# Dense experts: the products with the value rows' low halves move to the end of each output

## The chip, the cores and the metric

The kernel runs on one core of one Trainium2 chip. The metric is the device time of one execution in microseconds (us). The core has a matrix engine (TensorE, in the profile PE, with its weight loads as PEld), a vector engine (VectorE, DVE), an activation engine (ScalarE, ACT), a general engine (GpSimd, POOL) and an engine that issues transfers (SyncE, SP). Each works through its own queue in order, and semaphores tie the queues together.

## The reference

One inference step of a one-layer decoder: a prompt of 1024 tokens and 32 sample tokens go through attention, an RWKV mixer and a layer of 16384 single-neuron experts. The change concerns the experts (PEER), of which each token picks 16 for each of 8 heads:

```python
gate = jax.nn.softmax(top_s, axis=-1)
act = jax.nn.gelu(jnp.einsum('nd,nhkd->nhk', hb, expert_u[eid]).astype(jnp.float32), approximate=False)
return jnp.einsum('nhk,nhkd->nd', gate * act, expert_v[eid].astype(jnp.float32))
```

`eid` holds the 128 picked experts of each token. All data is float32.

## The kernel before

The layer's first half (projections, attention, RWKV) fills the first 1700 us or so and is not touched. For the experts the nine tiles of tokens (128 rows each, the last with the 32 sample tokens) are divided. Tiles 5, 6, 7 and the sample tile are *gathered*: for each picked expert GpSimd issues an indirect load of its rows (tile `row`), and VectorE multiplies and sums them. Tiles 0 to 4, 640 tokens, are *dense*: TensorE runs all 16384 experts over them, and a table of gates (`g`, zero where an expert is not picked) makes the result the same. Both streams run side by side, the gathered one with priority, the dense one as filling.

`dense` (line 1615) takes the experts in 128 blocks of 128, four blocks to a group (`NG`), so 32 groups. `hidden(b)` computes the hidden values of one block for all 640 tokens, 48 products with 320 columns, then gelu, gates, and a split into a high half `ch` and a low half `cl`. `values(grp, dh)` loads the value rows of the four blocks, for one half `dh` of the 1024 output columns: SP loads `v`, ACT casts it to the high half `vh`, and GpSimd (every eighth time VectorE) subtracts to get the low half `vl` (`split2`, line 1611). `v` has two buffers, `vh` and `vl` have five each. `output(grp, dh, tt)` adds the four blocks' products for one tile of tokens into one of four PSUM banks (`d`), and VectorE adds the bank to the accumulator `acc` (`dacc` in the profile). In a group come the hidden blocks, the values of the first half, five outputs, the values of the second half, and five more outputs. Float32 accuracy comes from three products per block, made by `mm3` (line 243): high by high, high by low, low by high:

```python
te.matmul(out, l[0], r[0], start=first, stop=False)   # ch by vh
te.matmul(out, l[0], r[1], start=False, stop=False)   # ch by vl
te.matmul(out, l[1], r[0], start=False, stop=last)    # cl by vh
```

The order of each engine's queue is not the order of the text: when the program is built, a planner with a table of expected durations puts at each step the most urgent instruction whose operands it expects to be ready into an engine's queue. Text order gives the urgency. The products of one output keep their order, since they add into the same bank. A buffer is handed on when the planner has seen its last reader, and the new writer waits for that reader on the chip. Almost every instruction of the kernel is recorded at line 196, a helper, so rows are told apart by their tiles.

Of the kernel before, what the change touches and what calls it, by code (L numbers as in the profile page):

```python
# [125 lines left out]
def _ap(t, offset, ap):  # L126
    return bass.AP(tensor=t.tensor, offset=t.offset + offset, ap=ap)
# [74 lines left out]
def tile_hybrid_step(ctx, tc, ins, outs):  # L202
# [3 lines left out]
    ve, sc, gp, te, sy = (_Metered(meter, n, e) for n, e in (("ve", nc.vector), ("sc", nc.scalar), ("gp", nc.gpsimd),  # L206
                                                               ("te", nc.tensor), ("sy", nc.sync)))
# [22 lines left out]
    def split(src, hi, lo, eng=None):  # L230

        sc.copy(hi, src)
        (eng or ve).tensor_tensor(lo, src, hi.bitcast(FT), op=OP.subtract)
# [9 lines left out]
    def mm3(out, l, r, first, last):  # L243

        if len(l) == 1:
            te.matmul(out, l[0], r[0], start=first, stop=last)
            return
        te.matmul(out, l[0], r[0], start=first, stop=False)
        te.matmul(out, l[0], r[1], start=False, stop=False)
        te.matmul(out, l[1], r[0], start=False, stop=last)  # L250
# [1360 lines left out]
    def split2(src, hi, lo, j):  # L1611
        sc.copy(hi, src)
        (gp if j in POOL_LO else ve).tensor_tensor(lo, src, hi.bitcast(FT), op=OP.subtract)

    def dense(pa, pp, acc, h2T, tiles):

        nt = len(tiles)
        n = 128 * nt
        NG = 4
        C_, V_, G_ = {}, {}, {}  # L1620
        gate2 = {}

        def hidden(b):
            uh = pa.tile([128, KD, 128], FR, tag="uh", name="uh", bufs=2)
            ul = pa.tile([128, KD, 128], FR, tag="ul", name="ul", bufs=2)
            for x in range(2):
                ks = slice(4 * x, 4 * x + 4)
                u = pa.tile([128, 4, 128], FT, tag="u", name="u", bufs=3)
                sy.dma_start(u, A["uT"][b, :, ks])
                split2(u, uh[:, ks], ul[:, ks], 8 + b % 2)  # L1630
            ch = pa.tile([128, n], FR, tag="ch", name="ch", bufs=NG + EARLY)
            cl = pa.tile([128, n], FR, tag="cl", name="cl", bufs=NG + EARLY)
            for h in range(2):
                if b % 4 == 0:
                    G_[h] = pa.tile([128, n // 64, 4, 32], FT, tag="g", name="g", bufs=3)
                    sy.dma_start(G_[h], g_d[n // 64 * h:n // 64 * (h + 1), :, b:b + 4].rearrange("s e i t -> e s i t"))
                cs = slice(h * n // 2, (h + 1) * n // 2)
                ps = pp("d")
                for k in range(KD):
                    mm3(ps[:, :n // 2], (uh[:, k], ul[:, k]), [x[:, k, cs] for x in h2T], k == 0, k == KD - 1)  # L1640

                t = ps[:, :n // 2]
                sc.activation(t, t, AF.Gelu)
                tv = t.rearrange("p (s t) -> p s t", t=32)
                ve.tensor_tensor(tv, tv, G_[h][:, :, b % 4], op=OP.mult)
                split(t, ch[:, cs], cl[:, cs])
            C_[b] = (ch, cl)

        def values(grp, dh):
            for b in range(NG * grp, NG * grp + NG):  # L1650
                v = pa.tile([128, 512], FT, tag="v", name="v", bufs=2)
                sy.dma_start(v, A["expert_v"][128 * b:128 * b + 128, 512 * dh:512 * dh + 512])
                vh = pa.tile([128, 512], FR, tag="vh", name="vh", bufs=5)
                vl = pa.tile([128, 512], FR, tag="vl", name="vl", bufs=5)
                split2(v, vh, vl, b % 8)
                V_[b, dh] = (vh, vl)

        def output(grp, dh, tt):
            ps = pp("d")
            for x in range(NG):  # L1660
                b = NG * grp + x
                mm3(ps, [c[:, 128 * tt:128 * tt + 128] for c in C_[b]], V_[b, dh], x == 0, x == NG - 1)
            if grp == 0:
                ve.tensor_copy(acc[:, tt, dh], ps)
            else:
                ve.tensor_tensor(acc[:, tt, dh], acc[:, tt, dh], ps, op=OP.add)
            if grp < ngrp - 1:
                return
            i, cs = tiles[tt], slice(512 * dh, 512 * dh + 512)
            if tt == 0:  # L1670
                gate2[dh] = pa.tile([128, 512], FT, tag="act", name="g2", bufs=2)
                sy.dma_start(gate2[dh], _ap(mod_d, 5 * D + 512 * dh, [[0, 128], [1, 512]]))
            x1 = pa.tile([128, 512], FT, tag="u", name="fx", bufs=3)
            sy.dma_start(x1, x1_d[i, :, cs])
            ve.tensor_tensor(acc[:, tt, dh], acc[:, tt, dh], gate2[dh], op=OP.mult)
            ve.tensor_tensor(x1, x1, acc[:, tt, dh], op=OP.add)
            sy.dma_start(outs["y_p"][128 * i:128 * (i + 1), cs], x1)

        ngrp = 128 // NG
        for b in range(EARLY):  # L1680
            hidden(b)
            yield
        for grp in range(ngrp):
            for b in range(NG * grp + EARLY, NG * grp + NG):
                hidden(b)
                yield
            values(grp, 0)
            for b in range(NG * (grp + 1), min(NG * (grp + 1) + EARLY, 128)):
                hidden(b)
                yield  # L1690
            for dh in range(2):
                if dh:
                    values(grp, 1)
                for tt in range(nt):
                    output(grp, dh, tt)
                    yield
# [303 lines left out]
```

## Time and profile before

| | us |
|---|---|
| median of 3 runs | 3760.14 (3759.74 to 3762.64) |
| profiled execution | 3753.1 |
| its span, first to last instruction | 3751.3 |
| PE busy in the span | 3453.9 (92%) |
| DVE busy | 2693.2 (72%) |
| POOL busy | 2080.6 (55%) |

Times in the views count from the span's start. "Idle" or a time in square brackets is what an engine stood still before an instruction, with an arrow to what released it. Matmuls overlap, so a PE row's own duration (0.39 us) is longer than the distance from one to the next.

### The profile page before, as it was taken

To read this page: it belongs to the slowest core of one execution; us is meant where nothing else is said; L and a number is where in the kernel's file an instruction comes from. 1 tells how busy PE (TensorE), PEld (TensorE's weight loads), DVE (VectorE), ACT (ScalarE), POOL (GpSimd) and SP (SyncE) were. 2 spreads that over 40 slices of the span, in tenths; PEclk is the share of its full clock that TensorE was granted. 3 is DMA by queue.
4 is the path that set the end of the run, shared out by engine and by line. 5 is a ranking of instruction groups with operands and counts; after the bars stand their busy time and mean duration, and the time that the engine had idled before them with its cause. 6 is when DMAs were issued, how large, how long until landed. Compare 5 with 4: busy or idle time off the path is not lost.

```text
span 3751.3 us, 57270 instructions
## 1 busy us (share of the span) xinstructions
PE 3453.9 (92%) x19618; PEld 2873.9 (77%) x19618; DVE 2693.2 (72%) x6059; ACT 1431.2 (38%) x3122; POOL 2080.6 (55%) x1842
## 2 busy tenths in 40 slices
PE   7999999789888988988999989999999999999998
PEld 3878678567767755556777778988888888898997
DVE  2556365588688656785778998787777877777787
ACT  5645345336765754543221122322223222222321
POOL 2342011015545446754655677777777777776784
PEclk8999999899999989998999999999999999999999
DMA  9653596553675568749988779999999999999997
GB/s 293 197 148 117 176 285 186 151 182 130 225 233 166 189 229 255 244 149 309 320 316 298 262 255 334 340 321 322 327 323 324 329 320 322 315 330 318 336 336 256
DMA packets 592528, 981.58 MB, mean 262 GB/s; under 512 B 78323, under 2 KB 354620, under 8 KB 589420
## 3 DMA queue, kind: packets, MB, share of 16 engines
q1 hardware_dynamic: 467788, 524.84, 43.9%
q0 software_dynamic: 124448, 453.08, 34.1%
q8 instruction: 155, 2.54, 0.3%
q14 instruction: 137, 1.12, 0.1%
HBM read 882.97 MB, written 94.78 MB: 261 GB/s over the span
## 4 chain that ended last, share of the span: by engine, by line
PE 51%; DMA 18%; DVE 14%; issue 7%; POOL 6%; ACT 3%; SPq 1%; POOLq 0%; DVEq 0%; ACTq 0%
PE d L196 23%; PE at L196 10%; PE rw L196 5%; PE pj L196 5%; DMA u<-in_uT 5%; PE rs L196 3%; POOL row L196 3%; DMA row<-in_expert_v,eid 3%; PE sp L196 2%; POOL vl L196 2%; DVE gh L196 2%; DVE ohb L196 1%; DMA v<-in_expert_v 1%; DMA w<-wq_d 1%; POOL ul L196 1%
## 5 line engine op out<-in xcount | busy, mean ns | idle before, releaser
L196 PE MATMUL d<-h2T,uh 128*128 128x320 f32 x4096 | 907.3, 311 | 18.1 <-DVE cl L196 9.0
L196 PEld LDWEIGHTS d<-h2T,uh 128*128 128x128 f32 x4096 | 689.6, 189 | 26.6 <-ACT h2T L196 8.2
L196 PE MATMUL d<-h2T,ul 128*128 128x320 f32 x2048 | 633.3, 311 | 0.6 <-POOL ul L196 0.6
L196 PE MATMUL d<-vl,ch 128*128 128x512 f32 x1280 | 508.3, 398 | 42.9 <-POOL vl L196 42.9
L196 DVE CUSTOM_DVE_ANT_0 row<-row,gh 128x1024 f32<-128x1024 f32 x416 | 500.4, 1215 | 63.5 <-DMA row<-in_expert_u,eid 50.7
L196 POOL DMA_INDIRECT row<-in_expert_u,eid x416 | 394.7, 949 | 242.0 <-DVE co L196 89.6
L196 PE MATMUL d<-vh,cl 128*128 128x512 f32 x1280 | 504.5, 395 | 0.0
L196 PE MATMUL d<-vh,ch 128*128 128x512 f32 x1280 | 478.3, 396 | 17.2 <-DVE cl L196 9.7
L196 POOL DMA_INDIRECT row<-in_expert_v,eid x416 | 397.1, 955 | 166.2 <-issue 46.2
L196 POOL TENSOR_SCALAR oha<-c_iota,tr 128x128 f32<-128x128 f32 x320 | 307.4, 966 | 312.1 <-PE sp L196 293.6
L196 POOL TENSOR_TENSOR ul<-u,uh 128x512 fp32r<-128x512 f32 x256 | 332.2, 1306 | 151.7 <-ACT uh L196 143.3
L196 ACT CAST vh<-v 128x512 fp32r<-128x512 f32 x256 | 158.8, 622 | 674.9 <-DMA v<-in_expert_v 451.9
L196 DVE SCALAR_TENSOR_TENSOR gh<-row,co,gh 128x1024 f32<-128x1024 f32 x285 | 366.1, 1285 | 48.6 <-DMA row<-in_expert_v,eid 46.7
L196 PEld LDWEIGHTS d<-h2T,ul 128*128 128x128 f32 x2048 | 386.2, 189 | 5.0 <-issue 3.7
L196 POOL TENSOR_TENSOR wl<-w,wh 128x1024 fp32r<-128x1024 f32 x50 | 123.0, 2461 | 387.2 <-ACT wh L196 326.8
L196 PEld LDWEIGHTS d<-vl,ch 128*128 128x128 f32 x1280 | 244.1, 191 | 108.0 <-POOL vl L196 58.6
L196 POOL TENSOR_TENSOR vl<-v,vh 128x512 fp32r<-128x512 f32 x224 | 289.0, 1301 | 45.7 <-ACT vh L196 42.7
L196 PEld LDWEIGHTS d<-vh,ch 128*128 128x128 f32 x1280 | 242.7, 190 | 77.5 <-DVE dacc L196 12.7
L196 ACT CAST uh<-u 128x512 fp32r<-128x512 f32 x256 | 154.8, 621 | 367.3 <-DMA u<-in_uT 212.2
L196 PEld LDWEIGHTS d<-vh,cl 128*128 128x128 f32 x1280 | 243.9, 191 | 52.8 <-issue 2.5
L196 DVE TENSOR_TENSOR dacc<-dacc,d 128x512 f32<-128x512 f32 x310 | 206.2, 683 | 47.8 <-PE d L196 47.6
L196 DVE TENSOR_TENSOR d<-d,g 128x320 f32<-128x320 f32 x256 | 126.8, 496 | 155.6 <-ACT d L196 142.4
(449 smaller groups left out, 6779.4 us busy)
## 6 DMA issues: line engine op xcount, KB each, us to landing
u<-in_uT SPq DMA_DIRECT2D x256, 256.0 KB
v<-in_expert_v SPq DMA_DIRECT2D x256, 256.0 KB
w<-wq_d SPq DMA_DIRECT2D x224, 256.0 KB
g_d<-stage SPq DMA_DIRECT2D x20, 2048.0 KB
g<-g_d SPq DMA_DIRECT2D x64, 640.0 KB
w<-in_w_in SPq DMA_DIRECT2D x75, 512.0 KB
w<-in_w_out SPq DMA_DIRECT2D x112, 256.0 KB
adaw<-in_ada_w SPq DMA_DIRECT2D x32, 512.0 KB
```

The lines of the kernel that those rows point to most:

```text
L196: return f(*a, **k)
```

## The change

In `output`, the call of `mm3` per block is replaced by two passes over the four blocks: in the first, each block's `ch` by `vh` and `cl` by `vh`; in the second, each block's `ch` by `vl`. The sum is the same apart from the order of its terms. No other function changes.

```diff
         def output(grp, dh, tt):
             ps = pp("d")
-            for x in range(NG):
-                b = NG * grp + x
-                mm3(ps, [c[:, 128 * tt:128 * tt + 128] for c in C_[b]], V_[b, dh], x == 0, x == NG - 1)
+
+            for part, x in [(0, x) for x in range(NG)] + [(1, x) for x in range(NG)]:
+                (ch, cl), (vh, vl) = C_[NG * grp + x], V_[NG * grp + x, dh]
+                ts = slice(128 * tt, 128 * tt + 128)
+                if part:
+                    te.matmul(ps, ch[:, ts], vl, start=False, stop=x == NG - 1)
+                else:
+                    te.matmul(ps, ch[:, ts], vh, start=x == 0, stop=False)
+                    te.matmul(ps, cl[:, ts], vh, start=False, stop=False)
             if grp == 0:
                 ve.tensor_copy(acc[:, tt, dh], ps)
```

## Rows read from the trace of the kernel before

**Rows 1.** The page: the span and each engine's busy time.

```profile
span 3751.3 us, 57270 instructions
PE 3453.9 (92%) x19618; PEld 2873.9 (77%) x19618; DVE 2693.2 (72%) x6059; ACT 1431.2 (38%) x3122; POOL 2080.6 (55%) x1842
```

**Rows 2.** Windows: length, each engine's busy time, clock, DMA share, GB/s.

```profile
core 0: us, PE busy (x) PEld busy (x) DVE busy (x) ACT busy (x) POOL busy (x), PEclk, DMA share, GB/s
3300.00:3500.00 200.00, 192.34 (x1076) 174.09 (x1075) 152.23 (x207) 55.41 (x113) 146.28 (x136) 0.99 0.94 326
```

**Rows 3.** Waits of PE's weight loads from 1700 on: total, times, longest.

```profile
PEld d L196 <- POOL vl L196: 58.6, 39, 3.3
PEld d L196 <- DVE dacc L196: 12.7, 16, 1.7
PEld d L196 <- ACT vh L196: 2.6, 3, 1.3
```

**Rows 4.** Timeline of PE in group 22: start, duration, instruction, idle time before.

```profile
3146.34 0.39 PE L196 MATMUL d<-vl,ch 128*128 128x512 f32 x1
3146.57 0.39 PE L196 MATMUL d<-vh,cl 128*128 128x512 f32 x1
...
3148.61 0.39 PE L196 MATMUL d<-vh,cl 128*128 128x512 f32 x1
...
3150.87 0.84 PE L196 MATMUL d<-vh,ch 128*128 128x512 f32 x3
3153.48 0.50 PE L196 MATMUL d<-vl,ch 128*128 128x512 f32 x1 [1.76 <-POOL vl L196]
...
3159.09 1.07 PE L196 MATMUL d<-vh,ch 128*128 128x512 f32 x4
3162.23 0.79 PE L196 MATMUL d<-vl,ch 128*128 128x512 f32 x1 [2.07 <-POOL vl L196]
3162.83 0.63 PE L196 MATMUL d<-vh,cl 128*128 128x512 f32 x1
3163.25 0.63 PE L196 MATMUL d<-vl,ch 128*128 128x512 f32 x1
```

**Rows 5.** Timeline of ACT in group 22: the second half's high halves.

```profile
3146.99 1.30 ACT L196 CAST vh<-v 128x512 fp32r<-128x512 f32 x2 [0.75 <-PE d L196]
3158.04 1.26 ACT L196 CAST vh<-v 128x512 fp32r<-128x512 f32 x2 [9.74 <-DMA v<-in_expert_v]
```

**Rows 6.** Timeline of POOL in group 22: low halves and what precedes them.

```profile
3152.16 2.50 POOL L196 TENSOR_TENSOR vl<-v,vh 128x512 fp32r<-128x512 f32 x2
...
3159.80 1.09 POOL L196 DMA_INDIRECT row<-in_expert_v,eid  x1 [0.31 <-issue]
3160.91 1.27 POOL L196 TENSOR_TENSOR vl<-v,vh 128x512 fp32r<-128x512 f32 x1
```

**Rows 7.** SP's timeline in group 22, and a window behind the second stop.

```profile
3153.45 9.08 SPq L196 DMA_DIRECT2D v<-in_expert_v  x4
...
3162.15:3165.56 3.41, 3.33 (x8) 2.65 (x9) 2.07 (x4) 0.00 (x0) 0.98 (x2) 0.50 1.00 398
```

**Rows 8.** Timelines (PE, ACT, POOL) of groups 8 and 32: first and last of 25.

```profile
2333.39 0.39 PE L196 MATMUL d<-vh,cl 128*128 128x512 f32 x1
2333.35 2.55 POOL L196 TENSOR_TENSOR vl<-v,vh 128x512 fp32r<-128x512 f32 x2
2339.00 0.63 ACT L196 CAST vh<-v 128x512 fp32r<-128x512 f32 x1 [5.92 <-DMA v<-in_expert_v]
2347.32 0.46 PE L196 MATMUL d<-h2T,uh 128*128 128x320 f32 x2
...
3725.94 0.39 PE L196 MATMUL d<-vh,cl 128*128 128x512 f32 x1
3731.42 0.62 ACT L196 CAST vh<-v 128x512 fp32r<-128x512 f32 x1 [5.75 <-DMA v<-in_expert_v]
3739.54 0.39 PE L196 MATMUL d<-vh,cl 128*128 128x512 f32 x1
```

**Rows 9.** The tile `row`: VectorE's sums, with first and last start.

```profile
L196 DVE SCALAR_TENSOR_TENSOR gh<-row,co,gh x285: 1268/1285/1304, 2065.4 to 3716.0; 128x1024 f32<-128x1024 f32 x143
```

## The prediction

> **What bounds the kernel now.** I read the page first: TensorE (PE) is busy for 92% of the span of 3751.3 us, ahead of VectorE and of GpSimd [rows 1]. Then I cut the second half into windows of 200 us. In one window PE works for 192 of 200 us at a granted clock of 0.99, and VectorE, GpSimd and the transfers are well filled too, the transfers to 0.94 [rows 2]. PE also runs the dense experts to the end: the last product of the dense stage starts at 3739.54, 12 us before the end of the span [rows 8], while the last sum over a gathered row starts at 3716.0 [rows 9]. So PE time that is saved or lost in the dense stage moves the end one for one, until about 20 us are saved. From there the gathered stream would end last.
>
> Next I asked what PE waits for in that stage. The largest item is the low halves of the value rows: 39 weight loads wait 58.6 us for vl from GpSimd, 3.3 us at most. The bank that VectorE has to empty costs 12.7 us in 16 waits. The high halves cost next to nothing, 2.6 us in three waits [rows 3]. Taken alone, these rows say that the change removes 58.6 us. The timeline of one group says where the waits come from, and it says otherwise.
>
> Group 22 is the pattern. I call the three products of a block H (ch by vh), L (ch by vl) and C (cl by vh). The first half's last product starts at 3148.61. The second half then runs H L C at a pitch of 0.23 us, with two stops. At 3150.87 three H stand alone, and the next L comes at 3153.48: it waited for vl of block 1. At 3159.09 four H stand alone, and the next L comes at 3162.23: it waited for vl of block 3 [rows 4]. Where L waits, the C of the same output waits behind it, although its operands are there. The products of one output keep their order, and all four banks are taken by outputs in the same position.
>
> Behind both stops is one chain of buffers. vh of blocks 1 and 2 is made at 3146.99, when the last output of the first half gives its buffers back [rows 5]. GpSimd makes vl of blocks 1 and 2 from 3152.16 to 3154.71, behind other work in its queue [rows 6]. Only then is one of the two buffers of v free, and the load of v of block 3 goes out at 3153.45 [rows 7]. It lands just before ACT starts vh of block 3 at 3158.04 [rows 5]. GpSimd makes vl of block 3 at 3160.91, after a gather [rows 6].
>
> **The change, part by part.** No product is added or removed. An output is still 12 products, of 0.2275 us each at the pitch of group 22, which is 2.73 us, and a half of five outputs is 13.65 us. The change touches only the order inside an output: H C of four blocks, then four L. I costed the second half of 25 groups, the 8th to the 32nd, since no work of the routed tiles' front end lies between their products. I read each from the timelines as I did group 22. The first of them runs from 2333.62 to 2347.32, the last from 3726.17 to 3739.77 [rows 8]. The 25 together take 406.3 us, against 25 x 13.65 = 341.3 us of pure products. So 65.1 us are lost today: waits for vl, waits for a bank, and stretches at half clock after a stop.
>
> Removed: all of these 65.1 us, because the next part counts every wait anew.
>
> Added, first term, the wait for vh of block 3. In the new order an output can run H and C of blocks 0 to 2 and must then have vh of block 3. Four banks hold four outputs, so PE has 4 x 6 = 24 products, 5.46 us, and then nothing to do. Before, it had 36 products ahead of that point. Measured from the end of the first half, vh of block 3 is ready after 4.7 to 11.0 us (mean 7.9, later than 5.46 in 23 of 25). In group 22 that is 3158.66 - 3148.83 = 9.83 us, a stop of 4.37 us. In group 8 the cast ends 6.0 us after, a stop of 0.55; in group 32 5.9 us after, a stop of 0.41 [rows 4, 5, 8]. The 25 stops sum to 61.5 us.
>
> The same in another way: today 20 products (8 of block 3 and 12 of the fifth output) are left once vl of block 3 is there. After the change 36 are left once vh of block 3 is there. The 16 more take 3.64 us. vl comes 1.4 to 4.65 us after vh, mean 2.8. So the new order ends the half earlier only where GpSimd is more than 3.64 us behind ACT, in 8 of the 25.
>
> The Trainium skill (Perfetto Trace Analysis, Optimization Strategy) says that the same gap repeating on the engine that should be full can mean that no memory is left to allocate the next tile. By that rule an order that adds no buffer keeps the gap and only moves it: 65 us in place of 65. Nothing below needs this; the rows' own figure for the moved gap is the 61.5 us just worked out, and they agree with the rule as far as the load at 3153.45 goes, which starts as vl of block 1 ends.
>
> Second term, vl of block 3 itself. After the stop PE has 8 products H and C and 12 L of blocks 0 to 2, 4.55 us, which covers the mean lag. If the build's planner queues the first output's last L after 10 products, the 25 halves lose 18.7 us more. If it queues it after 5, they lose 41.0 us more. If it comes last, nothing. The planner orders by what it expects to be ready, so I take 5 us.
>
> Third term, the clock. In group 22 the second stop is followed by 3.41 us at a granted clock of 0.50, which is the lower level, 1.2 GHz [rows 7]. Eight products then run at 0.42 us instead of 0.23, for instance from 3162.83 to 3163.25 [rows 4], a loss of 1.6 us. Of the 14 stops of over 2 us between 2100 and 3740, 10 were followed by such a stretch. The new order has one long stop in place of two short ones, over 2 us in 15 of the 25 groups. 15 x 10/14 = 11 stretches of 1.6 us make 17 us; the bounds are 10 and 24.
>
> Fourth term, the chain starts later. vl of block 1 needs the buffer that the first half's last output gives back with its L of block 0. That is its second product now, at 3146.34 in group 22, and its ninth then, 7 x 0.2275 = 1.6 us later, at 3147.93 [rows 4]. It needs vh too, which is made from 3146.99 to 3147.61 [rows 5] and comes a little earlier in the new order, since C is the second product instead of the third. So the earliest start moves back by about 0.7 us, and what is queued behind it on GpSimd, gathers above all, with it; the load of v of block 3 on SP follows. In most groups GpSimd is busy until later anyway: in group 22 until 3152.16 [rows 6]. I bound this by 0 and 25 x 0.7 = 17.5 us and take 7 us, near the lower end, as that row is far past the limit.
>
> Edits with no cost: the other half (its values are made while the hidden products run), the count of weight loads, VectorE's work per output. In the first seven groups other products fill the stops, so I take nothing there, with 5 us either way.
>
> Sum: -65.1 + 61.5 + 5 + 17 + 7 = +25 us. The profiled execution took 3753.1 us, 1.8 us more than its span; the sum gives 3778.5 there. The median of the three runs is 3760.1, 7 us above the profiled one; with the same sum it becomes **3785 us**.
>
> **Rivals.** *The waits for vl go and little takes their place (faster).* Mechanism: the planner puts vl of block 1 ahead of the gathers on GpSimd, so the load of v of block 3 goes out within a microsecond of the first half's end, as it does in group 8, where GpSimd starts that vl at 2333.35 [rows 8]. It decides where vh of block 3 arrives before 5.46 us. If every group were like groups 8 and 32, the stops would be 0.5 us each, 12 us instead of 65, a gain of 50; the gathered stream then ends last and cuts it to about 20 us: 3740 us. For it: groups 8 and 32. Against it: the median of the 25 is 8.2 us, and nothing in the change moves GpSimd's gathers.
>
> *An even trade (no change).* vl of block 3 is covered, the chain doesn't start later, and the clock falls as rarely as today (six stretches, 10 us): 61.5 + 10 - 65.1 = +6 us, 3766. For it: the two stops of a group and the one that replaces them hang on the same load.
>
> *Much slower.* The planner queues the last L early, and GpSimd waits for the late buffer in every group: 61.5 + 41 + 24 + 17.5 - 65.1 = +79 us, 3839. Against it: the four H in a row at 3159.09 show that it puts off what it takes to be late.
>
> That the change doesn't do what it says is not a case: the order inside an output is fixed by the bank it adds into.
>
> **How the numbers follow.** Forecast 3785 with a chance of 0.52; faster 0.14; even trade 0.20; much slower 0.14. A measurement of this kernel tells 0.2%, 7.5 us, from no change. Slower takes the forecast and the much slower case, 0.66. The range leaves out most of the faster case and the far half of the much slower one: 3748 to 3830.
>
> **What would show it.** Right: PE's waits for vl nearly gone; in their place a wait for vh of block 3 (or for its load) of some 2.5 us in each second half, after 24 products H C; more stretches at half clock. Wrong: no wait for vh of that size; vl of block 1 made much earlier than today; PE's waits for vl still there at the first L. If the new waits are as forecast and the time still doesn't rise, the dense stage isn't what ends last.

## The result and the profile after

The changed kernel takes 3790.35 us, median of 10 runs (3771.88 to 3795.06), beside 3763.01 us for the kernel before (10 runs, 3758.62 to 3775.46). The ratio is 1.0063 with a 95% interval of 1.0049 to 1.0078: **slower by 0.63%, about 24 us** (the medians lie 27 us apart). Its profiled execution took 3795.06 us, the longest of its runs, and that of before, 3753.1 us, lies below the bottom of the later runs. So the two first profiles differ by 42 us, more than the kernels do. Both were profiled once more below.

The page of the changed kernel, its first lines, answers to [rows 1]: PE works 11 us longer at a lower share of a longer span, and VectorE, ScalarE and GpSimd work as long as before to within 7 us.

```profile
span 3793.3 us, 57261 instructions
PE 3465.3 (91%) x19618; PEld 2881.7 (76%) x19618; DVE 2695.8 (71%) x6059; ACT 1424.3 (38%) x3124; POOL 2076.6 (55%) x1842
```

The waits of PE's weight loads from 1700 us on, in the changed kernel (total us, times, longest), answer to [rows 3]:

```profile
PEld d L196 <- DVE dacc L196: 46.1, 23, 3.3
...
PEld d L196 <- ACT vh L196: 34.8, 19, 3.6
...
PEld d L196 <- POOL vl L196: 2.0, 2, 1.3
```

The waits for vl are gone, from 58.6 us to 2.0. Two others have taken their place: vh of the value rows, from 2.6 to 34.8 us, and the banks that VectorE empties, from 12.7 to 46.1 us.

One group shows both. These are rows of PE's timeline in group 21 of the changed kernel (start, duration, instruction, idle time before); they answer to [rows 4].

```profile
3124.95 0.39 PE L196 MATMUL d<-vh,ch 128*128 128x512 f32 x1
...
3130.17 0.39 PE L196 MATMUL d<-vh,cl 128*128 128x512 f32 x1
3131.31 0.50 PE L196 MATMUL d<-vh,ch 128*128 128x512 f32 x1 [0.76 <-ACT vh L196]
...
3135.30 1.75 PE L196 MATMUL d<-vl,ch 128*128 128x512 f32 x7
3139.92 0.50 PE L196 MATMUL d<-vh,ch 128*128 128x512 f32 x1 [2.87 <-DVE dacc L196]
```

The second half starts at 3124.95. After 24 products H and C, at 3130.17 + 0.23, PE stands until ACT has made vh of block 3. Then come the rest, and at 3135.30 seven L in a row: blocks 0 to 2 of the fourth output, and then the last L of all four outputs, so that four banks are finished within 0.7 us. The fifth output needs one of them and starts only at 3139.92.

The same group on GpSimd and on ACT, which answers to [rows 5, 6]:

```profile
3125.43 2.55 POOL L196 TENSOR_TENSOR vl<-v,vh 128x512 fp32r<-128x512 f32 x2
...
3132.85 1.30 POOL L196 TENSOR_TENSOR vl<-v,vh 128x512 fp32r<-128x512 f32 x1
...
3122.89 1.14 ACT L196 CAST vh<-v 128x512 fp32r<-128x512 f32 x2 [1.19 <-PE d L196]
3130.64 0.62 ACT L196 CAST vh<-v 128x512 fp32r<-128x512 f32 x1 [6.62 <-DMA v<-in_expert_v]
```

vl of block 1 begins half a microsecond after the first half's end, where in [rows 6] it began 3.3 us after. vl of block 3 is done at 3134.15, when PE still has other products: no wait for it is left.

And VectorE, behind the seven L:

```profile
3138.03 1.22 DVE L196 CUSTOM_DVE_ANT_0 row<-row,gh 128x1024 f32<-128x1024 f32 x1 [1.18 <-DMA row<-in_expert_u,eid]
3139.18 0.08 DVE L196 DVE_READ_ACCUMULATOR2_ANT co<- 128x1 f32 x1
3139.18 2.47 DVE L196 TENSOR_TENSOR dacc<-dacc,d 128x512 f32<-128x512 f32 x4
```

The bank of the first output is complete by about 3136.4, when the fourth of the seven L ends. VectorE is free at 3136.9, but the next entry of its queue is a gathered row whose transfer lands at 3138. The four additions follow it in one piece.

For the 25 groups 8 to 32 I summed PE's stops from its timeline: the distance from one product's start to the next, less the pitch (0.2275 us, 0.1475 us in the hidden products). The products on both sides tell which stop it is. A stop ahead of an output's first H counts as bank; in the first profile of either kernel some 3 us of that column are waits for `cl` or vh. What the half clock costs is the same excess inside the stretches of granted clock 0.5. All times in us:

| kernel | groups 1-7 | groups 8-32 | vl | vh of block 3 | bank | half clock | median of the runs |
|---|---|---|---|---|---|---|---|
| before, first profile | 587.7 | 1447.9 | 44.7 | 0 | 8.2 | 8.9 | 3763.0 |
| before, second | 588.7 | 1447.6 | 44.6 | 0 | 5.5 | 12.0 | 3759.6 |
| changed, first | 599.1 | 1476.6 | 0 | 25.0 | 43.9 | 20.2 | 3790.4 |
| changed, second | 600.1 | 1454.2 | 0 | 19.1 | 39.8 | 8.4 | 3785.5 |

Some 6 to 8 us of small stops a row belong to no column. Most of them are the second product after a stop, which follows the first one later than the pitch (6.1 us in all in the first profile of the changed kernel). The waits by weight load put the vh column some 5 us higher, 30.5 instead of 25.0 in that profile.

### The profile page after: what moved, and what is told of

It reads as the page before. It is cut to its first block, busy times and chain, and to the rows that moved or that the text cites. A ratio compares the mean times of both kernels' runs of the same rounds, so it can differ in the third digit from the quotient of the medians.

```text
span 3793.3 us, 57261 instructions
## 1 busy us (share of the span) xinstructions
PE 3465.3 (91%) x19618; PEld 2881.7 (76%) x19618; DVE 2695.8 (71%) x6059; ACT 1424.3 (38%) x3124; POOL 2076.6 (55%) x1842
## 4 chain that ended last, share of the span: by engine, by line
PE 32%; DMA 10%; DVE 5%; POOL 4%; issue 4%; ACT 0%; SPq 0%; POOLq 0%; DVEq 0%; ACTq 0%
PE d L196 28%; DMA u<-in_uT 4%; PE at L196 4%; DMA row<-in_expert_v,eid 2%; DMA row<-in_expert_u,eid 2%; POOL row L196 2%; DVE gh L196 1%; POOL ul L196 1%; POOL vl L196 1%; DVE row L196 1%; DMA v<-in_expert_v 1%; DVE dacc L196 1%; DVE ga L196 0%; DMA g<-g_d 0%; DVE d L196 0%
## 5 line engine op out<-in xcount | busy, mean ns | idle before, releaser
L196 PE MATMUL d<-vh,ch 128*128 128x512 f32 x1280 | 517.9, 405 | 81.1 <-DVE dacc L196 36.2
L196 DVE CUSTOM_DVE_ANT_0 row<-row,gh 128x1024 f32<-128x1024 f32 x416 | 500.7, 1214 | 81.6 <-DMA row<-in_expert_u,eid 61.5
L196 PEld LDWEIGHTS d<-vh,ch 128*128 128x128 f32 x1280 | 246.0, 192 | 158.8 <-DVE dacc L196 46.1
L196 PE MATMUL d<-vl,ch 128*128 128x512 f32 x1280 | 355.1, 399 | 1.1 <-POOL vl L196 1.1
```

The costliest lines, as they stand in the source:

```text
L196: return f(*a, **k)
```

## The experiments

**Theory A** was that of the prediction, put right by this profile: stops behind buffers, and half clock behind the stops, make the time. **Theory B**: the order itself costs, through the products or through the way the planner shifts the two streams.

**A third buffer for v**, under the changed order and under the old one. The gate rows of the last group give the room.

```diff
-                v = pa.tile([128, 512], FT, tag="v", name="v", bufs=2)
+                v = pa.tile([128, 512], FT, tag="v", name="v", bufs=3)
-                gate2[dh] = pa.tile([128, 512], FT, tag="act", name="g2", bufs=2)
+                gate2[dh] = pa.tile([128, 512], FT, tag="act", name="g2", bufs=1)
```

> The changed kernel with three buffers for v instead of two (the gate rows of the last group get one buffer instead of two, to make room). Theory A: the new time comes from stops behind buffers: 31 us of waits for vh of block 3, whose load waits for a buffer of v, 44 us of waits for the bank of the fifth output, since four outputs end together on their last L, and stretches at half clock behind them. Then the third buffer takes the wait for vh of block 3 away, and with vl of block 3 made earlier also most of the bunched ends: 3715 to 3750 us, PE's waits for vh under 8 us. Theory B: the order itself costs the time (the planner shifts the two streams against each other, or the products run worse in this order), and the buffers only show it: still 3775 to 3790 us.

> The kernel before with the same third buffer for v. Theory A: the wait for vl of block 3 goes (about half of the 45 us of waits for vl in the 25 groups), the wait for vl of block 1 stays, since GpSimd still makes it behind gathers: 3730 to 3750 us, and slower than or equal to the changed kernel with three buffers. Theory B: faster than the changed kernel with three buffers by 20 us or more.

Measured: 3713.52 us with the changed order (ratio to before 0.9869, 0.9839 to 0.9898) and 3733.14 us with the old one (0.9918, 0.9894 to 0.9942). The changed order is the faster one here, a little under the range that I had given for it. PE's waits in the changed order with three buffers:

```profile
PEld d L196 <- DVE dacc L196: 11.4, 6, 4.2
...
PEld d L196 <- POOL ul L196: 2.4, 5, 0.8
```

No wait for vh or vl is among its rows, and the bank costs a quarter of the 46.1 us. The 25 groups take 1393.6 us (old order 1393.8). So the load that waited for a buffer of v made the stops, and Theory B fails: the order is no handicap where the buffer is there. With vl of block 3 early, the last L of the four outputs no longer stand together: the longest row of L ahead of the fifth output's has five instead of seven. That the bank wait falls to 6.9 us in the 25 groups, at the same work on VectorE, speaks for its being the four ends at once. In the old order the weight loads' waits for vl in the 25 groups fall from 52.4 to 8.5 us, further than the half that I had expected.

Both kernels now end on the other stream. VectorE's rows of the tile `row` in the changed order with three buffers:

```profile
L196 DVE SCALAR_TENSOR_TENSOR gh<-row,co,gh x285: 1261/1285/1292, 2071.3 to 3704.7; 128x1024 f32<-128x1024 f32 x143
```

Their last sum starts at 3704.7, while the last dense product ends at 3684.2. So the two kernels' 20 us are a difference between two gathered streams (3706.0 against 3726.7 at their ends), not between the orders in the dense stage.

**No low halves**: the product with vl reads vh, and the subtraction is left out, in either order.

```diff
-                vl = pa.tile([128, 512], FR, tag="vl", name="vl", bufs=5)
-                split2(v, vh, vl, b % 8)
-                V_[b, dh] = (vh, vl)
+                sc.copy(vh, v)
+                V_[b, dh] = (vh, vh)
```

> The changed order with no low halves: the product with vl reads vh in its place and GpSimd's subtraction for the value rows is left out, so no product waits for vl and a buffer of v is free as soon as ACT has cast it. The number of products is the same. Theory A: no stops are left, so the order costs nothing: within 8 us of the same kernel in the order of before, both 3690 to 3730 us. Theory B: 20 us or more slower than that one.

> The order of before with no low halves (the product with vl reads vh, the subtraction for the value rows is left out). Theory A: 3690 to 3730 us, within 8 us of the changed order without low halves. Theory B: the same time, but 20 us or more under the changed order.

Measured: 3721.15 us in the changed order (0.9882, 0.9856 to 0.9909), 3693.89 us in the old one (0.9819, 0.9796 to 0.9841). That is 27 us apart, as Theory B had it and not as I had expected. The waits of PE say why; first the changed order, then the old one:

```profile
PEld d L196 <- ACT vh L196: 45.6, 23, 3.1
```

```profile
PEld d L196 <- DVE dacc L196: 6.3, 5, 2.4
```

My "no stops are left" was wrong. A buffer of vh is now what the last L of the first half gives back late, and block 3's load waits for it through the buffer of v. With 24 products ahead, PE stands at H of block 3; with 36 ahead (old order) it never does. But the load isn't at the same place in the two: in the changed order it goes out 0.2 us after the first half's end, in the old one 1.15 us before it, and vh of block 3 is there 6.6 and 4.7 us after that end (means of the 25 groups). A replay adds up, over the 25 groups, what each arrival exceeds the products ahead by. 24 products (5.46 us) would cost 33.9 us with the changed order's arrivals and 3.4 us with the old order's; 36 (8.19 us) would cost next to nothing with either. It takes both, the late load and the shorter cover. In the 25 groups the two kernels take 1422.2 and 1383.3 us. Without their stops (40.2 and 4.8) and the half clock (3.0 and 0) they are at 1379.0 and 1378.5. The same subtraction gives 1380.0 for before, 1379.8 for the changed kernel, 1378.4 and 1378.8 for the two with three buffers. So products in the new order run as fast as in the old one. This pair shows the stop at vh with hardly any bank waits: 39 us in the 25 groups for 12 products fewer ahead of a load that also goes out 1.3 us later. In the profiles the first seven groups differ by another 19 us (566 and 586), which I can't place; and the old-order kernel's last gathered sum (3684.8) ends behind its dense stage (3656.1), so the 27 us of the medians are no measure of the dense stage alone.

**Additions into the accumulator first**, on VectorE.

```diff
+            with tc.high_priority(offset=2 * AHEAD):
+                if grp == 0:
+                    ve.tensor_copy(acc[:, tt, dh], ps)
+                else:
+                    ve.tensor_tensor(acc[:, tt, dh], acc[:, tt, dh], ps, op=OP.add)
```

> The changed kernel, with the additions of a finished bank into the accumulator given the gathered stream's priority, so that the planner queues them on VectorE as early as it can. Theory A (the fifth output waits for its bank because four outputs end together on their last L and VectorE has a sum over a gathered row queued ahead, which waits for its transfer): the wait of L to H falls from 44 us in the 25 groups to under 20, with fewer stretches at half clock, and the wait for vh of block 3 stays at about 31 us: 3755 to 3775 us. Theory B (the bank wait is what four ends within a microsecond cost on VectorE whatever its queue): no change, 3780 to 3795 us.

Measured: 3777.67 us (1.0046, 1.0028 to 1.0064), between the ranges of the two theories. The bank wait stays at 40.3 us in the 25 groups, so the urgency given to the planner doesn't cure it. In a group of this kernel (VectorE, then PE):

```profile
3060.31 1.29 DVE L196 SCALAR_TENSOR_TENSOR ga<-row,co,ga 128x1024 f32<-128x1024 f32 x1 [0.24 <-DMA row<-in_expert_v,eid]
3061.50 2.48 DVE L196 TENSOR_TENSOR dacc<-dacc,d 128x512 f32<-128x512 f32 x4
...
3062.24 0.50 PE L196 MATMUL d<-vh,ch 128*128 128x512 f32 x1 [1.52 <-DVE dacc L196]
```

A gathered row, for which VectorE still waits 0.24 us, goes ahead of the four additions: the edit didn't move them to the front of the queue, which was fixed when the program was built. So this run doesn't settle what the bank wait would be with VectorE free at once. The first profile of the changed kernel says how the two go together: in 15 of its 25 groups the weight load's wait is put down to the additions behind seven L in a row, and in all 15 VectorE comes from a gathered row straight to the first addition, which starts 0.9 to 2.5 us after the last L does.

**The new order in one half of a group only.** Part 2 stands for H L C of one block. The lines are those of the second-half kernel, shortened; the first-half kernel has `dh == 1` there.

```diff
+            seq = [(0, x) for x in range(NG)] + [(1, x) for x in range(NG)]
+            if dh == 0:
+                seq = [(2, x) for x in range(NG)]
...
```

> The new order in the second half of each group only; the first half keeps H L C. If the cost lies in the stops of the second half, as theory A has it, the time is that of the changed kernel, 3775 to 3795 us. The buffers of vl come back earlier than in the changed kernel, so GpSimd no longer waits for TensorE with vl of block 1 (87 us in the changed kernel). If that early return matters, vl of block 1 and the load behind it come at other times, and the wait for vh of block 3 moves towards the 61 us of the replay from before's times.

> The new order in the first half of each group only; the second half keeps H L C. Theory A: the second half has its old stops, for vl of blocks 1 and 3, and hardly any for vh; what the first half adds is that vl of block 1 can start 0.7 us later. 3755 to 3775 us. If the first half's order were what makes the changed kernel slower, 3780 us or more.

Measured: second half only 3765.45 us (1.0000, 0.9980 to 1.0020), first half only 3770.88 us (0.9996, 0.9976 to 1.0015). The second-half kernel has the stops of the changed kernel in the 25 groups, 30.4 us for vh and 30.8 for the bank, and none for vl; the first-half kernel has the old ones, 53.5 us for vl. So the kind of stop belongs to the second half's order. But Theory A's 3775 to 3795 us for the second-half kernel missed, and the sizes don't add up to the changed kernel's time: each alone costs nothing that can be measured, both together 24 us. In their profiles the 25 groups take 1459.8 and 1462.4 us, 12 and 15 us more than before, and the first seven 582.2 and 585.1, less than before's 587.7. The second-half kernel's 25 groups lie between the changed kernel's two profiles (1476.6 and 1454.2); what it lacks is the changed kernel's longer first seven groups, 17 us, and those I can't place. The early return of the buffers of vl, which I had thought could matter, doesn't bring the wait for vh to 61 us, and against my expectation GpSimd still waits for TensorE ahead of vl (49.9 us). What does differ is the load of v of block 3: it goes out 1.3 us after the first half's end in the second-half kernel and 3.3 us after in the first-half one (means of the 25 groups; before 2.8, changed 1.5). So vl of block 1 comes early with the second half's new order, not with the first half's. Why the planner does that is not shown.

**H C L in each block.**

```diff
+                te.matmul(ps, ch[:, ts], vh, start=x == 0, stop=False)
+                te.matmul(ps, cl[:, ts], vh, start=False, stop=False)
+                te.matmul(ps, ch[:, ts], vl, start=False, stop=x == NG - 1)
```

> Block by block as before, but H C L in each block instead of H L C. 36 products stay ahead of the first one that needs vh of block 3, so the wait for vh stays near zero. While vl is late the C products can run: the waits for vl in the 25 groups fall from 45 us to about 20. If the bank wait of the changed kernel comes from last products that stand together, it appears here too, since the four outputs now end in four L in a row: 15 to 40 us of waits for the bank, and the total lands between 3740 and 3770 us. If there is no bank wait: 3725 to 3745 us.

Measured: 3750.88 us (0.9963, 0.9939 to 0.9986). Its profiled execution was its longest, 3772.46 us, so I read only the kinds of its stops. For vl there are 16.6 us in the 25 groups, near zero for vh, and 40.5 for the bank: the four last L stand together again. PE in one group:

```profile
3065.99 1.21 PE L196 MATMUL d<-vl,ch 128*128 128x512 f32 x4 [0.53 <-POOL vl L196]
3069.48 0.50 PE L196 MATMUL d<-vh,ch 128*128 128x512 f32 x1 [2.27 <-DVE dacc L196]
```

The bank wait came as foretold, with 36 products ahead and no stop at vh. It goes with the four ends, not with the rest of the changed order.

**Both kernels once more**, for second profiles.

> The changed kernel once more, for a second profiled execution beside a second one of before. Theory A: in the 25 groups the stops are those of the first profile to within 10 us each: no wait for vl, 25 to 40 us for vh of block 3, 35 to 55 us for the fifth output's bank, over 10 us of half clock. If the first profile was only an unlucky execution, the stops are those of before. 3780 to 3795 us.

> The kernel before once more, for a second profiled execution. Theory A: waits for vl 40 to 55 us in the 25 groups, under 5 us for vh, 5 to 12 us for the bank, and the 25 groups 20 us or more shorter than in the changed kernel's profile of the same chip. 3755 to 3770 us.

Measured: changed 3785.52 us (1.0072, 1.0050 to 1.0095), before 3759.62 us (0.9990, 0.9975 to 1.0005). The table above has their stops. Kinds and sizes repeat. What doesn't is the half clock of the changed kernel, 20.2 us and 8.4 us, and with it the distance in the 25 groups, 28.7 us in the first pair of profiles and 6.6 us in the second. I had expected 20 us or more there. The first seven groups cost 11.4 us more in both pairs.

**L of blocks 0 to 2 ahead of block 3.**

```diff
-            for part, x in [(0, x) for x in range(NG)] + [(1, x) for x in range(NG)]:
+            seq = [(0, 0), (0, 1), (0, 2), (1, 0), (1, 1), (1, 2), (0, 3), (1, 3)]
+            for part, x in seq:
```

> H C of blocks 0 to 2, then L of blocks 0 to 2, then H C L of block 3: the low halves stand late, but all nine products of blocks 0 to 2 stay ahead of the one that needs vh of block 3, 36 for four outputs as in the kernel before instead of 24. Theory A: the wait for vh falls from 31 us in the 25 groups to under 5, the wait for vl stays under 20, and the bank wait stays at 30 us or more, since the last L of four outputs still stand together: 3740 to 3765 us, under the changed kernel by 25 us or more. If the order of the products costs the time by itself, it stays within 15 us of the changed kernel.

Measured: 3741.26 us (0.9945, 0.9924 to 0.9965), 44 us under the changed kernel's 3785.5 of the same chip, and 0.55% under before. Its waits:

```profile
PEld d L196 <- DVE dacc L196: 47.4, 28, 4.2
...
PEld d L196 <- POOL vl L196: 10.7, 11, 2.5
```

With the 36 products back ahead of H of block 3, the wait for vh is 3.8 us in the 25 groups (30.5 in the changed kernel), vl costs 10.7, and the bank wait stays, as the four last L stay (36.0 us by the timeline). vh of block 3 comes as late as in the changed kernel, 6.4 us after the first half's end beside 6.2 (means of the 25 groups). By the replay with its arrivals, 24 products ahead would cost 30.3 us and 36 would cost 4.1. So it is the cover that takes this wait away. These are the three parts of the theory in one kernel.

## Why the prediction was right

The forecast was 3785 us within 3748 to 3830, slower with a chance of 0.66; the time is 3790, slower by 24 us where the sum said +25. The mechanism carried in part: the stop at vl went, and a stop at vh of block 3 after 24 products came in its place. But it is less than half of what was forecast, and a wait of about the size that it lacks, for the banks, was not in the sum at all. These two errors of some 40 us each have opposite signs. That the time came within 6 us of the forecast is luck.

*What is removed* held. Waits for vl went from 58.6 to 2.0 us in all, from 44.7 to none in the 25 groups.

*First term, the wait for vh of block 3*: 61.5 us forecast; the timeline has 25.0 and 19.1 in the two profiles, the weight loads 30.5 and 24.7. PE did stop after exactly 24 products, and the sum over 25 groups with the arrivals measured after the change gives 23.7 and 18.1 us, so the reckoning with 5.46 us holds. What was mis-sized is when vh comes: I kept before's times, mean 7.9 us after the first half's end, and in the changed kernel it is 6.2 and 5.9.

*Fourth term* is why: the step that failed. I expected the late buffer to push vl of block 1 back by up to 0.7 us, and so the load. Its limit did move as worked out: the earliest ends of vl of block 1 lie at 0.91 to 0.93 us after the first half, in before at 0.16 to 0.20, and 13 of 25 sit at that limit. But on average it came earlier: it ends 1.5 and 1.4 us after the first half, in before 2.7 and 2.6, and the load of v of block 3 moves with it. GpSimd now stands and waits for TensorE ahead of vl, instead of making gathers first:

```profile
POOL vl L196 <- PE d L196: 100.2, 33, 24.0
```

In before no such wait is among GpSimd's. That is the mechanism of the faster rival, which I had given 0.14 because nothing seemed to move the gathers. It happened, with the second half's new order and not with the late buffer, as the kernels with one half changed show; and it didn't decide, since the stop shrank and did not go. It was also one of the signs that I had named for being wrong, as was a wait for vh below 2.5 us in each second half: it is 1.0 and 0.8 us. Both came in part, beside two signs of being right: the waits for vl nearly gone, and a wait for vh after 24 products. The gathered stream did not pay for it: its last sum ended at 3693.9 us, in before at 3717.3.

*Second term, vl of block 3*: 5 us forecast, 0 and 0.4 us measured as a wait for vl in the 25 groups. The planner put the last L last, as its four H in [rows 4] suggested.

*"Edits with no cost: VectorE's work per output"* is the step that is missing from the sum. The work is the same, the moments aren't: last L last means four banks that end within 0.7 us, and the fifth output waits for VectorE, 43.9 and 39.8 us in the 25 groups instead of 8.2 and 5.5. The seven L in a row were to be had from the second term's own case "if it comes last, nothing".

*Third term, the clock*: forecast 17 us in the 25 groups, with 10 as the lower bound; measured 20.2 and 8.4, beside 8.9 and 12.0 in before. In the second pair the clock costs less than before the change. The size of a stretch was right; how often a stop is followed by one differs between executions of the same kernel by more than I allowed.

*The first seven groups*: nothing forecast, 5 us either way; 11.4 us more in both pairs, which lies outside that allowance. In groups 5 to 7 of the first pair a stop at vh is new (6.2 us), the bank costs 5.4 us instead of 3.4, and the waits for vl fall from 5.3 to 1.1 us: that makes 4 of the 11.4. The rest stays open. The second-half kernel, the one with urgent additions and the changed order with three buffers take 581 to 582 us there, 17 to 18 less than the changed kernel, so it isn't the order of the products alone.

*The rivals*: the even trade fell with the interval of the ratio. The much slower case needed L queued early, which the planner didn't do. That the gathered stream ends last once the dense stage gains more than some 20 us, which capped the faster rival, shows in both kernels with three buffers.

## What to carry to other kernels

When an operand is late, ask which buffer its load waits for, and count the work that stands ahead of the first instruction that needs it. Moving other work behind that instruction takes cover away: here 36 products ahead became 24. Look too at what the new order makes end together: accumulation banks that finish at once must be emptied one after another, by an engine with a queue of its own. One buffer more for v was worth more than any order that was tried: with it the changed kernel takes 3713.5 us, 1.3% under before; the best order alone (L of blocks 0 to 2 ahead of block 3) gave 0.55%.

## What was not expected of the hardware

Executions of one and the same changed kernel differ by 23 us (3771.88 to 3795.06), and the two profiled ones have 20.2 and 8.4 us of half clock in the same 25 groups, with 68.9 and 58.9 us of stops at vh and the bank. Part of the spread lies ahead of the dense stage, in work that the change doesn't touch: the first dense product starts at 1704.0 and 1715.0 us in the two profiles of before, at 1706.1 and 1713.1 in those of the changed kernel. A queue that waits more can still end sooner: GpSimd waited 100 us for TensorE and its gathered sums were done 23 us earlier. The second profiles repeat it (3679.9 us beside 3729.9), the new order in the second half alone has it (3670.3), in the first half alone not (3736.2). Why is not shown.
